# A two-role hybrid layer on eight cores: the split of the sequence moved from row 2176 to 2240, tiles of 64 rows at the ends of the roles, recurrent weights issued ahead of the branch, the last rows finished by halves

## The chip, the cores and the metric

One Trainium2 chip, one program on all eight cores, on two dies (cores 0 to 3 and 4 to 7). The time of a run is the device time of the slowest core, in microseconds (us). Some executions fall into a slower state, whatever the kernel: the cores of a die then show a lower granted TensorE clock. Such runs are marked slow and left out; all comparisons are between fast runs. In the traces PE is the matrix engine (TensorE), DVE the VectorE, ACT the ScalarE, POOL GpSimd and SP SyncE.

## The reference, cut to what matters

Four sequences of 4096 rows, 1024 channels, one layer:

```python
def reference(x, ...):                                   # x (4, 4096, 1024) float32
    h = rmsnorm(x, norm_mix)
    proj = h @ w_in                                      # u_pool | u_rnn | u_gate | g_merge (2 x 1024)
    y_pool = pool_mixer(u_pool, ...) @ w_pool_out
    v  = causal_depthwise_conv(u_rnn, conv_w, conv_b)    # 4 taps
    hr = rg_lru(v, ...)                                  # gates r, i from 128x128 blocks, then the scan below
    y_rnn = (hr * gelu(u_gate)) @ w_rnn_out
    x = x + (g_merge[0] * y_pool + g_merge[1] * y_rnn) @ w_o
    gu = rmsnorm(x, norm_ffn) @ w_ffn_in                 # 1024 -> 2 x 2816
    x = x + (silu(gate) * up) @ w_ffn_out
    return rmsnorm(x, norm_final)

# rg_lru: a_t = sigmoid(lam)^(8 r_t);  h_t = a_t h_{t-1} + sqrt(1 - a_t^2) (i_t v_t)
```

The scan over rows is what ties the two halves of a sequence together.

## The kernel before

Each sequence has two cores. The even core (first role) does rows 0 to T1 in two passes. The odd core (second role) cannot have the first role's recurrent state in time, so it computes it again: for rows 0 to T1 it redoes the norm, the recurrent projection, the convolution, the gates and the scan (the stage called "pre"), and then does all the work for rows T1 to 4096 in two passes. (cuts are marked `# ...`)

```python
T1 = 2176

CFG0 = {'role': 'a', 'P': 0, 'T': 2176,
        'passes': [{'T': 1152, 'rnn': [...], 'ffn': [384, 384, 384], 'groups': [11, 11], ...},
                   {'T': 1024, 'norm': [342, 342, 340], 'rnn': [342, 342, 340], 'mm': [512, 512],
                    'ffn': [512, 512], 'gch': [[0, 512], [512, 1024]], 'groups': [11, 11], ...}], ...}
CFG1 = {'role': 'b', 'P': 2176, 'T': 1920, 'pre': [256, 384, 768, 768],
        'passes': [{'T': 896, ...}, {'T': 1024, 'norm': [512, 512], 'rnn': [512, 512], 'ffn': [512, 512], ...}], ...}
```

The order of all instructions on all engines is not written by hand. Every operation is put down once with the buffers that it reads and writes; a scheduler in the program then simulates the engines and, where several operations could start, takes the one with the lowest rank. The ranks of some thousand operations of each role were found by a search with that simulation as the objective, and stand in the file as two packed tables:

```python
            tab = np.frombuffer(zlib.decompress(base64.b85decode(cfg["table"])), np.int32).reshape(2, -1)
            for o, r, q in zip(g.ops, *np.cumsum(tab, axis=1, dtype=np.int32)):
                o.rank = int(r) / 100.0
                o.gate = None if o.gate is None else int(q) / 100.0
        self.sched = Schedule(g, cfg["opts"])
```

One unit of the recurrence (one block of 128 channels by n rows; the names in the traces are those of the tiles here):

```python
        def rnn_unit(grp, j, wu, h, c0, n, rank, own, ...):
            # PE:   bu  = projection of h (n + 4 columns) by wu
            # ACT:  v   = first tap of the convolution
            # DVE:  v  += three more taps                     (L887 before, L928 after)
            # POOL: vb  = bf16 copy of v
            # PE:   ba, bx = two gates of vb                  (ps<-vb,rg)
            # ACT:  w = tanh(bx); a = tanh(ba); a = exp(a)    (L900, L903, L906; after: L941, L944, L947)
            # DVE:  w = (w + 1) * v
            # ACT:  v = a * a; v = sqrt(1 - v)                (tables: tanh, exp, sqrt)
            # DVE:  v = v * w; w = scan(a, v)                 (the scan of 768 columns takes 1.81 us, a product 0.96)
            # POOL: hst = last column of w
            # own rows only, DVE or POOL: gate the result into rt
```

The head of the program, the same for both roles, then the branch. The first body (near) is the second role's, the taken branch (far) goes to the first role's:

```python
        first_weights(range(2), -98)
        # ...
        norm_chunk(first, 16, 0, 256, -90, True, (1, 3, 5))
        g.pro = False                              # from here on: behind the branch
        g.grp = ("start",)
        first_weights(range(2, 8), -80)            # the other six recurrent weights
        load(cbr, dr["cbr"], 4096, -10)            # read by nobody in this configuration
        # ...
                e.br_eq(r, 0, far, near)
```

The end of the last pass, for each tile of 128 rows:

```python
                    for c in range(2):
                        bk = psum()
                        # PE:  11 matmuls, stationary Act[:, off:off+128], moving w2[:, c*512:(c+1)*512]
                        # DVE: X[t][:, c*512:(c+1)*512] += bk
                    if last:
                        rs = inv_root(X[t], ...)   # ACT square with sum over 1024 columns, two POOL steps
                        # DVE: X[t] = X[t] * rs * gF (1024 columns);  SP: store of X[t]
```

## Time and profile before

| | before |
|---|---|
| median of 3 runs | 1051.06 us (1047.61 to 1191.61; the last is a slow run) |
| spans of the even cores (first role) | 989.5 to 996.2 us, clock .985 to .989 |
| spans of the odd cores (second role) | 1041.9 to 1044.9 us, clock .966 to .968 |
| PE work of core 5, from the shapes (each matmul N / 2.4 GHz + 2.5 ns, a float32 one twice the N; warm-up matmuls left out) | 921.1 us |
| PE time lost on odd cores after the first matmul, mean | 96.9 us: 83.0 before 200 us, 13.9 after |
| the same on even cores, missing records added | 38.6 us |
| from the last matmul to the end, odd / even | 15.5 / 9.7 us |

"PE time lost" is the sum over all matmuls of (start of the next minus start of this, minus the work of this one): waits and slow clock together. (The float32 ones of 128 columns start 112 ns apart in the trace. The warm-up matmuls, which keep PE busy where it would stand, count as work here: 6.9 us on odd cores, 11.2 on even ones. Where a trace lacks records of matmuls, their work would count as lost; on two of the four even cores 67 are missing, 14.5 us by their shapes, and this is taken off.)

### The profile page before, as it was taken

What the parts mean: (1) busy time and instruction counts of PE and PEld (TensorE: products, weight loads), DVE (VectorE), ACT (ScalarE), POOL (GpSimd) and SP (SyncE); (2) the same over time, 40 slices, a digit from 0 to 9 for tenths busy, and PEclk for the clock granted to TensorE, in tenths of its full rate; (3) what the DMA queues carried; (4) which work ended last, traced back from release to release, by engine and by line L of the source; (5) the groups of instructions that cost most, each with busy time, mean ns of one, the idle gap of its engine ahead of it and who ended that gap; (6) DMA issues with size and microseconds to landing.
All of it is one profiled execution on the core that took longest, in us unless ns stands there. A gap on an engine that the chain in (4) does not pass through costs nothing.

```text
span 1044.9 us, 13923 instructions; the slowest of 8 cores (989.5 to 1044.9 us)
## 1 busy us (share of the span) xinstructions
PE 966.0 (92%) x5012; PEld 486.0 (47%) x5012; DVE 644.7 (62%) x935; ACT 522.8 (50%) x808; POOL 282.8 (27%) x528
## 2 busy tenths in 40 slices
PE   6766887699999999999999999999999999999994
PEld 4544543244454555544444554444444444444441
DVE  1778898869888863545967776444464333533343
ACT  4999978999956543348645453231224311200012
POOL 5253422426314334300133222112423221000001
PEclk9979898899999999999999999999999999999997
DMA  9944000726827599920078455438993494000013
GB/s 223 278 130 122 1 1 0 131 31 109 118 67 126 102 242 303 216 41 11 1 121 141 61 86 126 73 70 201 191 163 70 63 190 80 1 11 1 1 41 124
DMA packets 48927, 106.26 MB, mean 102 GB/s; under 512 B 5203, under 2 KB 7635, under 8 KB 48852
## 3 DMA queue, kind: packets, MB, share of 16 engines
q0 software_dynamic: 34848, 63.45, 37.0%
q1 hardware_dynamic: 14004, 41.83, 11.9%
q8 instruction: 44, 0.72, 0.3%
q14 instruction: 31, 0.25, 0.1%
HBM read 160.84 MB, written 7.86 MB: 161 GB/s over the span
## 4 chain that ended last, share of the span: by engine, by line
PE 75%; ACT 14%; DMA 5%; issue 2%; POOL 1%; DVE 1%; SPq 0%; POOLq 0%; ACTq 0%
PE ps L834 47%; PE ps L1227 13%; PE ps L1154 5%; PE ps L1116 5%; PE ps L1110 2%; ACT v L883 2%; ACT v L919 2%; ACT a L906 2%; ACT w L900 2%; ACT a L903 2%; DMA wu<-win 1%; ACT v L917 1%; DMA wo<-wo 1%; ACT L919 1%; DMA gr<-win 1%
## 5 line engine op out<-in xcount | busy, mean ns | idle before, releaser
L887 DVE SCALAR_TENSOR_TENSOR v<-ps,con,v 128x768 f32<-128x768 f32 (+4 forms) x192 | 136.7, 744 | 35.7 <-ACT v L883 34.3
L834 PE MATMUL ps<-h,fu 128*128 128x512 bf16 (+1 forms) x704 | 151.4, 366 | 0.0
L834 PE MATMUL ps<-h,fg 128*128 128x512 bf16 (+1 forms) x704 | 150.5, 366 | 0.4 <-DMA fg<-fi 0.3
L1227 PE MATMUL ps<-w,act 128*128 128x512 bf16 x660 | 145.9, 379 | 0.0
L1207 ACT ACTIVATE th<-ps 128x512 f32<-128x512 f32 (+1 forms) x88 | 50.1, 571 | 151.2 <-PE ps L834 148.9
L1210 DVE SCALAR_TENSOR_TENSOR th<-th,ps 128x512 f32<-128x512 f32 (+1 forms) x88 | 57.0, 652 | 84.5 <-ACT th L1207 84.2
L834 PEld LDWEIGHTS ps<-h,fu 128*128 128x128 bf16 x704 | 68.7, 98 | 72.8 <-issue 1.2
L834 PEld LDWEIGHTS ps<-h,fg 128*128 128x128 bf16 x704 | 68.4, 98 | 73.1 <-issue 2.0
L1227 PEld LDWEIGHTS ps<-w,act 128*128 128x128 bf16 x660 | 64.3, 98 | 77.0 <-issue 0.2
L692 ACT ACTIVATE junk<-X 128x1024 bf16<-128x1024 f32 x30 | 31.7, 1057 | 133.7 <-DVE X L1231 88.0
L891 POOL CAST vb<-v 128x768 bf16<-128x768 f32 (+4 forms) x64 | 47.1, 737 | 176.6 <-DVE v L887 175.9
L1231 DVE SCALAR_TENSOR_TENSOR X<-ps,X 128x512 f32<-128x512 f32 x60 | 41.4, 690 | 83.5 <-PE ps L1227 83.5
L923 DVE TENSOR_TENSOR_SCAN w<-a,hst,v 128x768 f32<-128x768 f32 (+4 forms) x64 | 80.1, 1276 | 0.4 <-POOL hst L926 0.3
L1213 DVE TENSOR_TENSOR act<-th,ps 128x512 bf16<-128x512 f32 (+1 forms) x88 | 56.5, 652 | 38.0 <-PE ps L834 36.9
L926 POOL COPY hst<-w 128x1 f32<-128x1 f32 x64 | 34.7, 543 | 146.1 <-DVE w L923 144.9
L834 PE MATMUL ps<-h,wu 128*128 128x452 bf16 (+3 forms) x448 | 70.1, 303 | 4.4 <-DMA wu<-win 3.0
L834 PE MATMUL ps<-hp,wu 128*128 128x260 bf16 (+2 forms) x320 | 64.6, 363 | 6.0 <-ACT a L903 2.1
L883 ACT ACTIVATE v<-ps,con 128x768 f32<-128x768 f32 (+4 forms) x64 | 49.4, 785 | 40.5 <-PE ps L834 29.0
L695 POOL TENSOR_SCALAR rs<-rs 128x1 f32<-128x1 f32 x62 | 16.6, 267 | 169.0 <-ACT junk L692 166.2
L834 PE MATMUL ps<-h,gp 128*128 128x448 bf16 (+1 forms) x256 | 56.4, 368 | 3.1 <-ACT tp L1106 1.7
L910 DVE SCALAR_TENSOR_TENSOR w<-w,v 128x768 f32<-128x768 f32 (+4 forms) x64 | 44.4, 696 | 22.6 <-ACT w L900 21.8
L1116 PE MATMUL ps<-R,ro 128*128 128x448 bf16 (+1 forms) x256 | 55.4, 366 | 1.8 <-DMA ro<-ro 1.8
(102 smaller groups left out, 1512.7 us busy)
## 6 DMA issues: line engine op xcount, KB each, us to landing
nat<-x SPq DMA_DIRECT2D x32, 512.0 KB, 9.8
fg<-fi POOLq DMA_DIRECT2D x44, 256.0 KB, 6.5
w<-fo POOLq DMA_DIRECT2D x44, 256.0 KB, 7.8
fu<-fi POOLq DMA_DIRECT2D x44, 256.0 KB, 8.4
X<-x SPq DMA_DIRECT2D x15, 512.0 KB, 6.1
out<-X SPq DMA_DIRECT2D x15, 512.0 KB, 4.2
wu<-win POOLq DMA_DIRECT2D x16, 256.0 KB, 9.8
ro<-ro POOLq DMA_DIRECT2D x16, 256.0 KB, 6.6
```

The source lines that it names most:

```text
L834: ins.append(e.matmul(ap(bk)[:, q:m], lhsT=ap(wt)[:, kc * 128:(kc + 1) * 128], rhs=ap(h)[:, kc, c0 + q:c0 + m], start=(kc == 0), stop=(kc ...
L883: g.op("act", lambda e: [e.activation(out=ap(v)[:], in_=ap(bu)[:, 1:1 + n], func=AF.Identity, scale=cwk(0), bias=ap(con)[:, C_CB + j:C_CB ...
L887: g.op("dve", lambda e, k=k: [e.scalar_tensor_tensor(out=ap(v)[:], in0=ap(bu)[:, 1 + k:1 + k + n], scalar=cwk(k), in1=ap(v)[:], op0=ALU.mu ...
L891: g.op("pool", lambda e: [e.tensor_copy(out=ap(vb)[:], in_=ap(v)[:])], r=[v], w=[vb], dur=d_pool(n), rank=rank + 0.4, tag="vb", two=True)
L910: g.op("dve", lambda e: [e.scalar_tensor_tensor(out=ap(w)[:], in0=ap(w)[:], scalar=1.0, in1=ap(vp)[:, 0:n], op0=ALU.add, op1=ALU.mult)], r ...
L923: g.op("dve", lambda e: [e.tensor_tensor_scan(out=ap(w)[:], data0=ap(a)[:], data1=ap(v)[:], initial=ap(hst)[:, j:j + 1], op0=ALU.mult, op1 ...
L1116: g.op("pe", lambda e: [e.matmul(ap(byr)[:, 0:n], lhsT=ap(wro)[:, j * 128:(j + 1) * 128], rhs=ap(Rt[j])[:, a:b], start=(j == 0), stop=(j = ...
L1154: g.op("pe", lambda e, bk=bk, t=t, c=c: [e.matmul(ap(bk)[:], lhsT=ap(Mx[m])[:, t * 128:(t + 1) * 128], rhs=ap(wo[m])[:, c * 512:(c + 1) * ...
L1207: g.op("act", lambda e, bg=bg, n=n, th=th: [e.activation(out=ap(th)[:], in_=ap(bg)[:, 0:n], func=AF.Tanh, scale=0.5)], r=[bg], w=[th], dur ...
L1210: g.op("dve", lambda e, bg=bg, n=n, th=th: [e.scalar_tensor_tensor(out=ap(th)[:], in0=ap(th)[:], scalar=1.0, in1=ap(bg)[:, 0:n], op0=ALU.a ...
L1213: g.op("dve", lambda e, bu=bu, n=n, th=th, at=at: [e.tensor_tensor(out=ap(at)[:], in0=ap(th)[:], in1=ap(bu)[:, 0:n], op=ALU.mult)], r=[th, ...
L1227: g.op("pe", lambda e, bk=bk, t=t, c=c, ci=ci, off=off, f0=f0, nf=nf, Act=Act, w2=w2: [e.matmul(ap(bk)[:], lhsT=ap(Act[f, ci])[:, off:off ...
```

## The change

The intent: the second role is the longer one by some 50 us, so 64 rows go from it to the first role. Since 2240 is no multiple of 128, the last tile of rows of each role has 64 rows. The start of the first role is helped by issuing the six later recurrent weights ahead of the branch, and the end of both by finishing the last tile in two halves. The model inside the scheduler was refined (a clock gate for PE, the real cost of the branch for the first role, two DMA queues that share), and both tables of ranks were searched anew. The core of the diff (tables, model and the many `[0:m_]` slices cut):

```diff
-T1 = 2176
+T1 = 2240
...
         norm_chunk(first, 16, 0, 256, -90, True, (1, 3, 5))
+        g.grp = ("start",)
+        first_weights(range(2, 8), -89)
         g.pro = False
-        g.grp = ("start",)
-        first_weights(range(2, 8), -80)
-        load(cbr, dr["cbr"], 4096, -10)
...
+        load(cbr, dr["cbr"], 4096, -10)
...
-            nt = TA // 128
+            nt = (TA + 127) // 128
+            rows = [min(128, TA - 128 * t) for t in range(nt)]
...
-                            ap(bk)[:], lhsT=ap(Act[f, ci])[:, off:off + 128], rhs=ap(w2[f - f0])[:, c * 512:(c + 1) * 512],
+                            ap(bk)[0:m_], lhsT=ap(Act[f, ci])[:, off:off + m_], rhs=ap(w2[f - f0])[:, c * 512:(c + 1) * 512],
...
+                    if last and pi == len(cfg["passes"]) - 1 and t == nt - 1:
+                        for c in range(2):         # square of each half as soon as it is there
+                            ...
+                        for c in range(2):         # scale and store each half
+                            ...
+                    elif last:
...
 CFG0: 
- 'T': 2176,
+ 'T': 2240,
-             'groups': [11, 11],
+             'groups': [8, 7, 7],                              (both passes)
-            {'T': 1024, 'norm': [342, 342, 340], 'rnn': [342, 342, 340], 'mm': [512, 512], 'ffn': [512, 512],
+            {'T': 1088, 'norm': [384, 384, 320], 'rnn': [364, 364, 360], 'mm': [384, 384, 320], 'ffn': [384, 384, 320],
 CFG1: 
- 'P': 2176, 'T': 1920, 'pre': [256, 384, 768, 768],
+ 'P': 2240, 'T': 1856, 'pre': [256, 384, 768, 832],
-            {'T': 1024, 'norm': [512, 512], 'rnn': [512, 512], ...
+            {'T': 960, 'norm': [512, 448], 'rnn': [480, 480], ...
 (new "opts" and new rank tables for both roles)
```

## The prediction

> **What bounds the kernel now.** I read the spans of the cores first, because the time is that of the slowest of eight.
>
> ```profile
> core 0: 989.5 us, clock 0.989
> core 1: 1041.9 us, clock 0.968
> core 2: 993.3 us, clock 0.987
> core 3: 1042.8 us, clock 0.968
> core 4: 991.1 us, clock 0.989
> core 5: 1044.9 us, clock 0.967
> core 6: 996.2 us, clock 0.985
> core 7: 1044.1 us, clock 0.966
> ```
>
> Even cores (first role, rows 0 to T1) end some 50 us before odd cores (second role: it redoes norm, recurrent projection, gates and scan for rows 0 to T1, the "pre" stage, then all work for the rest). The two dies are alike, so this is imbalance and not the slow state. Only a shorter second role shortens the kernel, and the first role can take about half of the 50 us before it is the bound.
>
> Second, the 40 slices of core 5 (26 us each):
>
> ```profile
> PE   6766887699999999999999999999999999999994
> DVE  1778898869888863545967776444464333533343
> ACT  4999978999956543348645453231224311200012
> PEclk9979898899999999999999999999999999999997
> ```
>
> The first eight slices have holes in PE while DVE and ACT stand at 8 to 9: there the pre stage is bound by these two. After that PE is full. Core 0 has such holes in its first two or three slices only.
>
> Third, what a matmul costs. Ends of matmuls are modelled, so I take starts. In the timeline of core 0:
>
> ```profile
> 434.30 9.66 PE L1227 MATMUL ps<-w,act 128*128 128x512 bf16 x44
> 443.79 0.31 PE L894 MATMUL ps<-vb,rg 128*128 128x342 bf16 x1
> ...
> 451.72 1.46 PE L834 MATMUL ps<-h,fu 128*128 128x384 bf16 x8
> 453.02 1.33 PE L834 MATMUL ps<-h,wu 128*128 128x344 bf16 x8
> ```
>
> (443.79-434.30)/44 = 215.7 ns for 512 columns; (453.02-451.72)/8 = 162.5 ns for 384. Both are N/2.4 GHz + 2.5 ns. With that, the list of shapes gives the PE work: 930 us on core 0, 921 us on core 5. Summing over the trace by which starts exceed this leaves, after the first matmul at 3.3 us, 36 us of lost PE time on core 0 (31 of it in the first 100 us) and 98 us on core 5: 84 in the first 200 us, 14 later.
>
> Fourth, starts, in the timelines: GpSimd of core 0, then of core 5.
>
> ```profile
> 8.02 0.54 POOL L625 DMA_DIRECT2D wu<-win  x1
> 18.25 1.70 POOL L625 DMA_DIRECT2D wu<-win  x3 [6.06 <-issue]
> ```
>
> ```profile
> 7.07 0.54 POOL L625 DMA_DIRECT2D wu<-win  x1
> 11.18 3.29 POOL L625 DMA_DIRECT2D wu<-win  x6
> ```
>
> The six later recurrent weights are issued behind the branch on the role. On core 0 GpSimd idles 6.06 us there and issues at 18.25; core 5 goes on at once at 11.18. On core 0 PE then waits 6.3 us in all for wu.
>
> **What the Trainium skill says.** (1) "TensorE: Matmul & The Clock Gate", section "Wait — 56ns, not 53.3ns?": start to start a warm matmul takes N / 2.4 GHz plus about 2.5 ns, a cold one N / 1.2 GHz. The trace agrees: 215.7 and 162.5 ns. So a chunk of 384 instead of 512 columns costs only the 2.5 ns more often. (2) Same page, section "LDWEIGHTS (loading the stationary operand)": its time follows the columns of the weights. Together: where the tile of rows is the stationary operand (W_o and the FFN output, 512 columns moving), 64 rows take the matmul time of 128. No run so far has a 64-row tile. (3) "Runtime: NRT & Kernel Launch", section "Instruction fetch mechanics": a taken branch to a target outside the fetched pages makes the engine fetch before it goes on. The 6.06 us on core 0 fits; core 5 falls into the near body and shows none. (4) "DMA: Bandwidth & Descriptors", section "Issuing engines are not separate DMA queues": an earlier issue gains only if the shared engines have room. In the first 25 us their share is 0.82 on core 0 and 0.94 on core 5, so there is a little room on core 0.
>
> **The change part by part.** *First role, pass 2 from 1024 to 1088 rows* (chunks 512,512 to 384,384,320), PE time:
> - FFN in, 352 weight blocks: 2 x 215.8 = 431.7 ns per block becomes 162.5 + 162.5 + 135.8 = 460.8 ns. +29.2 x 352 = +10.3 us.
> - gate, both merge gates and recurrent out, 256 blocks: +29.2 x 256 = +7.5 us.
> - pooling projection and its output (32 + 32 blocks): +1.9. Recurrent projection (64 blocks) and gates (16): 64 columns more each, +1.7 and +0.4.
> - W_o: a ninth tile of rows at full price, 16 x 215.8 ns = +3.5 us. FFN out: 44 x 215.8 ns = +9.5 us. Transposes and norm +0.4.
>
> Sum +35.2 us, all on PE, which has no room after 100 us. If 64 rows cost half on the last two it would be 6.5 us less.
>
> *Second role, pass 2 from 1024 to 960 rows*: FFN in -352 x 26.7 ns = -9.4; the 256 blocks -6.8; pooling two -1.7; recurrent projection -2.0 (480+4 columns fit one matmul, 512+4 needed two); gates -0.4. W_o and FFN out: eight tiles before, seven and a half after, so still eight matmul sets, 0. Sum -20.3 us on PE-bound ground.
>
> *Second role, pre stage plus 64 rows* (its last chunk 768 to 832). PE adds 3 us, but PE has holes there. DVE decides: three taps, two products and a scan at two columns' time is 7 times 64/960 us for each of 8 channel blocks, 3.7 us, and 0.3 for normed columns. ACT: six passes x 8 x 64 x 0.83 ns = 2.6, and one more tile of squares (1.06 + 0.19) and 0.2: 4.0. These two are filled to about 90%, so the stage ends +4 us later. Net for the second role -16.3 us.
>
> *Weights ahead of the branch*: first role only, issue about 6 us earlier. The wait of 6.3 us shrinks and part of the cold stretch after it (granted clock 0.73 from 25 to 50 us) goes with it, but the DMA bytes and DVE and ACT limit what follows. I take -5 of the 31 us lost there. Second role 0: it had no gap.
>
> *Last rows by halves*: today after the last matmul come 0.69 (add), 1.25 (square), 0.22 and 0.57 (GpSimd), 1.28 (scale), then a store. The square of the first half moves under the last matmuls: 512 x 0.83 ns = 0.4 us less. Scale and store in halves may gain some tenths for the store, but on core 5 the scale ends at 1033.8, the queue sees the store at about 1035.7 and then waits another 7.8 us for the closing barrier, where GpSimd's drain, 8.9 us, is the late one. So -0.5 us at most.
>
> *Moved without PE cost*: groups of 8, 7, 7 instead of 11, 11 FFN blocks in the first role add one add per half tile and pass: 18 x 0.69 = 12 us of DVE per pass, where DVE stands at 3 to 8 tenths: hidden. They free buffers earlier. New ranks reorder both programs, searched with a model of the clock gate and of the slow branch. After 200 us the second role loses 14 us of PE time, mostly to late weights (fg, ro, gr, wo); I give the new order 3 of these.
>
> Sum, slowest core of each role: first 996.2 + 35.2 - 5 - 0.5 = 1026; second 1044.9 - 16.3 - 0.5 - 3 = 1025. The two meet. The time of a run lay 1.6 us over the longest span (1046.52 against 1044.9), which makes 1027; as the search may find somewhat more I say **1026 us**.
>
> **The rivals.** (a) The first role becomes the bound: if the early weights bring nothing (DMA busy anyway) and the extra DVE adds delay its recurrent stage of pass 2, it is 996 + 35 + 3 = 1034, so about 1035 us. For it: DVE is at 21 to 22 of 25 us on core 0 from 425 to 475 us, where pass 1's FFN and the second recurrence overlap. Against it: PE lost almost nothing there. (b) The pre stage is what the second role waits for, and a larger last chunk (832 columns, two PSUM banks, longer scans) costs more than its share, some 8 us: second role 1030, time 1031. For it: the 84 us lost. (c) The reordering does more than the rebalance: the schedule was searched before without the real cost of the branch and without the clock. If the pre stage and the start give up 10 us each, about 1016. Against: DVE and ACT are truly full there, and no operation is taken from them. (d) Only the imbalance matters and 64-row tiles were free: 1020.
>
> **Range and chances.** Rebalance alone gives 1028 to 1031, the small parts take 2 to 8 off. Eight times in ten the time lies between 1016 and 1036. Two per cent below the fast runs of before (1047.6 and 1051.1, mean 1049.3) is 1028.3, just above my figure: faster by over 2% 0.55, within 2% 0.43, slower by over 2% 0.02, as that needs a mishap in the order on a role that has 20 us in hand.
>
> **What would show it.** Spans of even and odd cores within about 10 us of each other, even 1018 to 1030, odd 1018 to 1030. W_o and FFN out matmuls 288 and 792 on even cores (272 and 748 now) with 512 columns, starts still 216 ns apart in the 64-row tile. On the odd cores unchanged, 240 and 660. GpSimd's wu loads on core 0 all issued before 16 us, the wait for wu under 3 us. On odd cores PE full from about 203 instead of 199 us. The closing wait of some 8 us still there. It would be wrong if 64-row tiles ran their matmuls faster, if even cores gained new PE holes in the middle, or if the holes of the first 200 us on odd cores shrank by more than 5 us.

## More of the kernel before

The prediction shows the spans, the slices of core 5 and the timelines of the starts. Three more views of before are needed for the comparison later. First the PE waits of core 5 from 200 to 300 us. Columns: who waited, for whom, total us, times, longest.

```profile
PE ps L834 <- ACT tp L1106: 1.7, 1, 1.7
PE ps L834 <- ACT a L903: 1.3, 1, 1.3
PE ps L834 <- ACT w L900: 0.6, 1, 0.6
```

Once the pre stage is over, next to nothing stops PE. Second, where it ends, in the PE timeline of core 5 (start, us, what, count; in brackets the idle time before and what ended it):

```profile
184.19 2.77 PE L834 MATMUL ps<-hp,wu 128*128 128x512 bf16 x16 [1.32 <-ACT a L903]
...
195.09 0.80 PE L897 MATMUL ps<-vb,rg 128*128 128x512 bf16 x2 [5.85 <-ACT w L900]
...
198.85 2.65 PE L834 MATMUL ps<-h,wu 128*128 128x452 bf16 x8 [0.44 <-ACT w L900]
```

`hp` are the redone rows, `h` the role's own. The last redone projection is at 184 us; the first one of own rows (452 columns) comes just before the last redone gates. So on PE the two kinds of work hardly mix: its last gates of a redone unit are at 202 us, and its own projections begin at 199. (DVE goes on with redone scans to 261 us.)

Third, the first stretches of core 5 by engine (columns: stretch, its length, then busy time and number of instructions of PE, weight loads, DVE, ACT, POOL, then clock, DMA share, GB/s):

```profile
0.00:50.00 50.00, 35.95 (x227) 24.50 (x228) 24.09 (x59) 34.77 (x69) 20.84 (x51) 0.94 0.97 247
50.00:100.00 50.00, 35.21 (x200) 23.57 (x198) 39.78 (x67) 49.85 (x88) 20.35 (x44) 0.86 0.49 145
200.00:250.00 50.00, 49.42 (x257) 24.82 (x256) 38.93 (x50) 48.40 (x72) 13.72 (x23) 0.99 0.37 62
```

ACT is busy all the time from 50 to 100 us; PE is nearly full from 200 us on.

## The result, and the profile after

| | before | after |
|---|---|---|
| fast runs | 1051.06, 1047.61, 1047.11 us | 1037.28, 1037.87, 1035.3 us |
| slow runs | 1191.61 us | 1156.55 us (clock .86 to .87 on die 0) |
| median of all four | 1049.34 us | 1037.57 us |

The ratio of the fast runs is 0.989 (95% interval 0.985 to 0.993): faster, but by 1.1%, less than two per cent. Ratios here are computed as the mean time of one kernel's fast runs over that of the other's of the same rounds, so they are not quite the ratio of the medians.

The spans of the cores after:

```profile
core 0: 1026.8 us, clock 0.987
core 1: 1035.6 us, clock 0.970
core 2: 1026.7 us, clock 0.988
core 3: 1031.4 us, clock 0.974
core 4: 1028.6 us, clock 0.985
core 5: 1031.6 us, clock 0.975
core 6: 1028.9 us, clock 0.983
core 7: 1031.9 us, clock 0.975
```

The two roles have met, as intended. Over the fast runs the even cores have a mean of 1028.6 us and the odd ones 1032.4. In a later session with both kernels in the same rounds (told below) the first role grew by 39.5 us and the second fell by 11.7; against the kernel before of the other sessions (even 990.3 to 991.8, odd 1044.0 to 1045.9, three chips) the first session's means give about +37.7 and -12. Predicted were +29.7 and -19.8. Single odd cores spread with a standard deviation of 2.1 us, and the slowest of four sets the time: in fast runs after, the slowest odd core has a mean of 1035.2 us, and the run lasts 1.65 us longer than that.

The forty slices of core 5 after (25.8 us each):

```profile
PE   6677867688999999999999999999999999999994
...
DVE  2577798978989877433676875484435534334353
ACT  3999869989986535334573753251214322001011
PEclk9989998899999999999999999999999999999998
```

The PE row has two more slices below nine tenths than before: the ninth and the tenth, 206 to 258 us. DVE falls back in the second slice (5 for 7). The waits of PE on core 5 from 200 to 300 us:

```profile
PE ps L875 <- DVE v L928: 2.5, 1, 2.5
PE ps L875 <- DMA wg<-win: 1.9, 1, 1.9
PE ps L935 <- ACT w L941: 1.7, 1, 1.7
PE ps L935 <- ACT R L1039: 1.4, 1, 1.4
PE ps L938 <- DVE v L928: 1.2, 1, 1.2
...
```

With two more lines of 1.0 and 0.2 these are 9.9 us, where before had 3.6. And the PE timeline of core 5:

```profile
137.87 1.69 PE L875 MATMUL ps<-h,wu 128*128 128x452 bf16 x8 [1.63 <-ACT w L941]
...
213.93 0.51 PE L938 MATMUL ps<-vb,rg 128*128 128x512 bf16 x2 [1.16 <-DVE v L928]
...
224.50 1.67 PE L875 MATMUL ps<-h,wg 128*128 128x448 bf16 x8 [1.89 <-DMA wg<-win]
...
229.85 2.99 PE L875 MATMUL ps<-hp,wu 128*128 128x512 bf16 x16
...
```

The new order mixes the two kinds of units. The first own projection is at 138 us instead of 199, the last redone one at 230 instead of 184, and PE's last gates of a redone unit at 263 instead of 202. So PE's part of the redone units, for which it waits on DVE and ACT, now stands among the projections of own rows, which before ran almost without a wait. The prediction let the redone stage end 4 us later ("so the stage ends +4 us later"); its last scan ends at 291 us on core 5, where it ended at 261. The first stretches by engine:

```profile
0.00:50.00 50.00, 34.19 (x215) 24.16 (x215) 19.46 (x49) 32.21 (x62) 20.48 (x50) 0.97 0.83 193
50.00:100.00 50.00, 36.17 (x193) 23.04 (x194) 36.73 (x59) 49.88 (x92) 27.86 (x60) 0.86 0.32 115
200.00:250.00 50.00, 45.54 (x227) 22.21 (x228) 42.30 (x44) 45.83 (x62) 27.40 (x34) 0.94 0.55 85
```

By 100 us DVE has done 56.2 us of work instead of 63.9, and from 200 to 250 us PE is busy for 45.5 us instead of 49.4. The mean lost PE time of the odd cores: 83.6 us before 200 us (83.0 before the change), 12.7 from 200 to 300 (5.0), 8.6 later (8.9); in all 104.9 instead of 96.9. Most of the growth lies from 200 to 250 us: 7.9 us against 1.4.

The even cores: 45.8 us lost instead of 38.6, with the missing records taken off as above (here 42 on two of the four, 9.1 us). The first 250 us got better, 28.7 instead of 34.8; after 250 us the loss went from 3.8 to 17.1. (Warm-up matmuls, which count as work, fell by 4.6 us besides.) The longest PE waits of core 0 after 250 us, where the kernel before had a single one of 1.2 us:

```profile
PE ps L875 <- DMA wu<-win: 2.5, 1, 2.5
PE ps L875 <- DVE th L1252: 2.5, 1, 2.5
PE ps L1270 <- ACT tp L1147: 2.1, 1, 2.1
...
```

The tile of 64 rows, in the groups by shape of core 0 (columns: count, busy us, mean ns of one, idle before):

```profile
L1270 PE MATMUL ps<-w,act 128*128 128x512 bf16 x718 | 163.6, 379 | 3.9 <-ACT tp L1147 2.1 <-DVE act L1255 0.2 <-issue 0.2
L1196 PE MATMUL ps<-wo,mx 128*128 128x512 bf16 x263 | 60.0, 379 | 0.5
...
L1270 PE MATMUL ps<-w,act 128*64 128x512 bf16 x44 | 10.2, 380 | 0.0
...
L1196 PE MATMUL ps<-wo,mx 128*64 128x512 bf16 x16 | 3.8, 382 | 0.0
```

With 64 stationary columns a matmul takes what it takes with 128; the starts in the tile of 64 rows lie 216 ns apart too. (Loads of 64 weight columns took 110 ns on core 5, those of 128 columns 98: that the load time follows the columns, as the prediction's second point has it, isn't seen here.) The end of core 5:

```profile
1016.86 0.63 ACT L1285 ACTIVATE junk<-X 64x512 bf16<-64x512 f32 x1 [1.33 <-DVE X L1274]
...
1019.24 0.63 ACT L1285 ACTIVATE junk<-X 64x512 bf16<-64x512 f32 x1 [1.65 <-DVE X L1274]
...
1021.16 1.41 DVE L1299 SCALAR_TENSOR_TENSOR X<-X,rs,gF 64x512 f32<-64x512 f32 x2 [1.96 <-POOL rs L1293]
1021.98 1.14 SPq L1303 DMA_DIRECT2D out<-X  x2
```

The first half's square lies under the last matmuls, and only 0.63 us of square is left behind them (1.06 before). From the last matmul to the end odd cores now take 13.4 us (15.5 before), even ones 7.5 (9.7).

### The profile page after: what moved, and what is told of

Read it like the earlier page. It is cut to its first block, busy times and chain, and to the rows that moved or that the text cites. A ratio compares the mean times of both kernels' runs of the same rounds, so it can differ in the third digit from the quotient of the medians.

```text
span 1035.6 us, 13703 instructions; the slowest of 8 cores (1026.7 to 1035.6 us)
## 1 busy us (share of the span) xinstructions
PE 952.9 (92%) x4906; PEld 487.1 (47%) x4906; DVE 640.6 (62%) x936; ACT 512.4 (49%) x806; POOL 286.7 (28%) x529
## 3 DMA queue, kind: packets, MB, share of 16 engines
q1 hardware_dynamic: 13956, 41.04, 11.6%
## 4 chain that ended last, share of the span: by engine, by line
PE 67%; ACT 15%; DVE 6%; DMA 5%; issue 3%; POOL 3%; SPq 0%; POOLq 0%; ACTq 0%
PE ps L875 44%; PE ps L1270 11%; PE ps L1157 5%; PE ps L1196 3%; PE ps L1151 2%; DVE v L928 2%; ACT v L960 2%; ACT a L944 2%; ACT a L947 2%; ACT v L924 2%; DMA nat<-x 2%; ACT junk L732 2%; ACT w L941 1%; ACT v L958 1%; PE ps L808 1%
## 5 line engine op out<-in xcount | busy, mean ns | idle before, releaser
L928 DVE SCALAR_TENSOR_TENSOR v<-ps,con,v 128x480 f32<-128x480 f32 (+5 forms) x192 | 137.9, 744 | 28.9 <-ACT v L924 27.5
L875 PE MATMUL ps<-h,fg 128*128 128x512 bf16 (+2 forms) x704 | 146.5, 359 | 1.8 <-DMA fg<-fi 1.8
L875 PE MATMUL ps<-h,fu 128*128 128x512 bf16 (+2 forms) x704 | 147.0, 359 | 0.2
L1270 PE MATMUL ps<-w,act 128*128 128x512 bf16 (+1 forms) x660 | 146.7, 379 | 0.0
L1252 DVE SCALAR_TENSOR_TENSOR th<-th,ps 128x512 f32<-128x512 f32 (+2 forms) x88 | 55.4, 635 | 90.9 <-ACT th L1249 90.6
L1270 PEld LDWEIGHTS ps<-w,act 128*128 128x128 bf16 (+1 forms) x660 | 64.8, 99 | 77.1 <-issue 1.7
L1255 DVE TENSOR_TENSOR act<-th,ps 128x512 bf16<-128x512 f32 (+2 forms) x88 | 55.3, 635 | 57.2 <-PE ps L875 56.2
L964 DVE TENSOR_TENSOR_SCAN w<-a,hst,v 128x448 f32<-128x448 f32 (+5 forms) x64 | 81.2, 1283 | 0.2
L875 PE MATMUL ps<-hp,wu 128*128 128x512 bf16 (+3 forms) x320 | 66.6, 367 | 7.7 <-DVE v L928 4.0
L875 PE MATMUL ps<-h,wu 128*128 128x484 bf16 (+2 forms) x320 | 64.6, 347 | 6.5 <-ACT w L941 3.2
L967 POOL COPY hst<-w 128x1 f32<-128x1 f32 x64 | 28.7, 449 | 127.3 <-DVE w L964 126.0
L875 PE MATMUL ps<-h,wg 128*128 128x448 bf16 (+1 forms) x256 | 56.3, 369 | 2.6 <-DMA wg<-win 2.5
L951 DVE SCALAR_TENSOR_TENSOR w<-w,v 128x480 f32<-128x480 f32 (+5 forms) x64 | 44.5, 697 | 20.5 <-ACT w L941 20.4
```

What stands on the lines that cost most here:

```text
L875: ins.append(e.matmul(ap(bk)[:, q:m], lhsT=ap(wt)[:, kc * 128:(kc + 1) * 128], rhs=ap(h)[:, kc, c0 + q:c0 + m], start=(kc == 0), stop=(kc ...
L928: g.op("dve", lambda e, k=k: [e.scalar_tensor_tensor(out=ap(v)[:], in0=ap(bu)[:, 1 + k:1 + k + n], scalar=cwk(k), in1=ap(v)[:], op0=ALU.mu ...
L951: g.op("dve", lambda e: [e.scalar_tensor_tensor(out=ap(w)[:], in0=ap(w)[:], scalar=1.0, in1=ap(vp)[:, 0:n], op0=ALU.add, op1=ALU.mult)], r ...
L964: g.op("dve", lambda e: [e.tensor_tensor_scan(out=ap(w)[:], data0=ap(a)[:], data1=ap(v)[:], initial=ap(hst)[:, j:j + 1], op0=ALU.mult, op1 ...
L1252: g.op("dve", lambda e, bg=bg, n=n, th=th: [e.scalar_tensor_tensor(out=ap(th)[:], in0=ap(th)[:], scalar=1.0, in1=ap(bg)[:, 0:n], op0=ALU.a ...
L1255: g.op("dve", lambda e, bu=bu, n=n, th=th, at=at: [e.tensor_tensor(out=ap(at)[:], in0=ap(th)[:], in1=ap(bu)[:, 0:n], op=ALU.mult)], r=[th, ...
```

## The experiments

Where the second role's missing eight us went had several candidates, and the runs were chosen between them.

- **The order** (the theory that stood at the end): the searched order mixes own units with redone ones and does more of ACT's other work early. The redone stage ends later, and its waits stop PE at 200 to 300 us, where PE would have been full.
- **The size**: the last redone chunk of 832 columns costs more than its share of 4 us.
- **The front**: the dead load `cbr` and early squares of the role's own rows hold up ACT and DVE in the first 100 us.
- **The weights**: gate weights are issued later (201 us against 183 on core 5), and PE waits for them.
- **The crowd**: the early recurrent weights compete with the second role's first rows for the DMA engines.

Each run is told as the mean span of even and odd cores over its fast runs, beside the kernel before of the same rounds (b) or the changed kernel's own first session (even 1028.6, odd 1032.4). The mean of the odd cores of one kernel has a standard error of 0.2 to 1.1 us, so differences under about 1 us decide nothing. Kernels that compute something wrong are marked; they must be read with more care: in one of them, told below, cores whose code is unedited ran at a clock of 0.983 instead of 0.986.

### Early weights put behind the branch again (correct, ratio 0.990)

```diff
+        for o in self.sched.order["pool"][9:16]:     # the six wu loads and the rest of rg
+            o.pro = False
```

> The changed kernel with six of the eight recurrent weight tiles and the second piece of the gate weights issued after the branch again, in the same order, as in the kernel before; nothing else is touched. My step said that their place ahead of the branch is worth 5 us to the first role and nothing to the second. Expected if that holds: even cores 5 us longer (mean of the profiled spans 1027.8 to about 1033), odd cores within 1 us of 1032.6. Rival C (the early weights crowd the second role's start and cause its lost time): odd cores 3 us or more shorter.

Measured: even 1032.0 (+3.4), odd 1032.7 (+0.3); b 990.3 and 1044.0. GpSimd of core 0 in the changed kernel, then in this one:

```profile
11.21 0.63 POOL L665 DMA_DIRECT2D wu<-win  x1
12.36 2.65 POOL L665 DMA_DIRECT2D wu<-win  x5
```

```profile
18.63 0.63 POOL L665 DMA_DIRECT2D wu<-win  x1 [5.71 <-issue]
19.79 2.65 POOL L665 DMA_DIRECT2D wu<-win  x5
```

The branch's 5.71 us stand in front of the loads again, and PE of core 0 then waits 9.4 us for wu in the first 60 us, against none in the changed kernel. The three runs told below on the same chip in the same rounds, which leave the first role as it is in the changed kernel, have even cores of 1028.2 to 1029.2, some 3.2 us less than here. So the early issue is worth some 3.4 us to the first role, and no effect on the second is seen: the crowd falls. Because the slowest core is an odd one, it is worth next to nothing to the time (ratio 0.990 against 0.989).

### The last tile finished whole (correct, ratio 0.990)

```diff
-                    if last and pi == len(cfg["passes"]) - 1 and t == nt - 1:
+                    if False:
```

> The changed kernel with its last row tile finished whole (one square over 1024 columns, one scale, one store), as in the kernel before; the rest untouched. My prediction had given the halves 0.5 us. In the traces the time from the last matmul to the end of the span fell by about 2 us on both roles (odd cores 15.5 to 13.4, even cores 9.7 to 7.5). If the halves made that: all cores 2 us longer (odd 1032.4 to about 1034.4, even 1028.6 to about 1030.6). If it came from the smaller last tile of 64 rows instead: 0.5 us or less.

Measured: even 1029.2 (+0.5), odd 1033.7 (+1.2); b 991.4 and 1045.2. In its trace the square behind the last matmuls is again one of 1.06 us on 64 rows, as half the rows don't make an ACT instruction shorter. The traces decide how much of the shorter end is due to the halves, since the spans are from two sessions and their differences near the error: from the last matmul's start to the end it is 13.9 us on odd cores and 8.0 on even ones, against 13.7 and 7.7 with halves. So the halves give 0.2 to 0.3 us of the some 2 us by which the end got shorter; the rest was not taken apart. (GpSimd's closing drain, told at the end, is as short here as in the changed kernel.)

### The dead load moved to 200 us (correct, ratio 0.990)

```diff
-        load(cbr, dr["cbr"], 4096, -10)
+        load(cbr, dr["cbr"], 4096, -10, gate=(200 if P else None))
```

In the second role's table only the rank and the gate of this load change. In the changed kernel its queue issues `cbr` and then stands for 3.6 us before the next rows are loaded.

> The changed kernel with one load moved: the convolution bias row, which no instruction of either role reads, is issued late by the second role instead of fourth, right ahead of the 384-row chunk's row loads; every other instruction keeps its place and its address, and the first role is untouched. In the changed kernel the first of those row loads waits 3.6 us for the dead load to land and the row loads leave at 8.3 to 9.0 us, against 4.0 in the kernel before; VectorE is then 3 to 4 us behind at 35 to 55 us. Theory A (the new order costs the second role its gain): the row loads leave at about 5 us, the odd cores get 2 to 4 us shorter (mean of the profiled spans 1032.6 to about 1029.5) and the even cores stay within 0.5 us of 1027.8. Rival B (64 more rows in the recurrence's last chunk cost about 8 us by themselves): no change on the odd cores. Rival C (the early weights crowd the start): the row loads leave earlier but land no sooner, so no change either.

Measured: even 1029.2, odd 1031.7 with a standard error of 1.0; b 990.3 and 1044.0. In the trace the first scans end 2 to 3 us earlier (the fourth at 52 us instead of 55, the thirteenth at 107 instead of 110), and so do most up to 300 us, and the lost PE time is 101.9 us instead of 104.9; the spans gained only 0.7 us, which isn't told from nothing.

### The last redone chunk worked on 64 columns less (ratio 0.988)

```diff
+            thin = [v, vb, a, w]
+            if grp[:2] == ("pre", 3):
+                n = n - 64                       # views of these four tiles, same order, same buffers
```

The state that the second role starts from then skips 64 rows, which is wrong by design; the decay of the recurrence keeps the outputs within tolerance.

> The changed kernel with the recurrent units of the second role's last redone chunk working on 768 of their 832 columns; all tiles, addresses and the order stay as they are. The result is wrong on purpose (64 rows are left out of the recurrence). From the rows of the trace one unit saves some 64 columns on each of 6 ScalarE and 7 VectorE instructions, so about 4 us of each engine over 8 units, and about 2 us of TensorE. Theory A (the order, not the size, costs the gain): the odd cores get at most 4 us shorter, the price that I had put on the size (1032.6 to about 1029). Rival B (the size itself costs about 8 us, through waits that it lengthens): the odd cores get about 8 us shorter, 1032.6 to about 1025. Even cores unchanged.

Measured: even 1028.2, odd 1030.5, that is 2.0 us less than the changed kernel, or 1.8 if each is taken against the kernel before of the same rounds (-13.5 here, -11.7 in the session told below). The prediction gives 64 columns in this stage 4 us. They are worth less than that, not more: PE's work fell by 2.1 us, and its lost time stayed (104.7 us). Nothing here speaks for a chunk that costs 8.

### Seven early squares of own rows cut to 16 columns (wrong, ratio 0.988)

```diff
-            rs = inv_root(nats[t], rank, "sq1")
+            rs = inv_root(nats[t], rank, "sq1", w=16 if P and P <= 128 * t < P + 896 else D)
```

ACT of core 5 does 23 squares of rows in the first 100 us, against 17 before the change.

> The changed kernel with the squares of the seven row tiles that belong to the second role's own first pass cut from 1024 columns to 16; the order stays. The result is wrong on purpose (those rows get a wrong norm). In the changed kernel ScalarE is busy without a break from 25 to 100 us and executes 23 squares in the first 100 us, where the kernel before had executed 17; each takes about 1.1 us. Theory A (these squares were pulled ahead of the recurrent units and starve VectorE, which falls from 3 us behind at 75 us to 7.7 behind at 100): VectorE catches up some 5 us by 100 us and the odd cores get 4 to 6 us shorter, 1032.6 to about 1028. Rival B (the size of the last chunk): no more than 1 us. Even cores unchanged.

Measured: even 1029.0, odd 1030.6 (1.9 less than the changed kernel); b 990.3 and 1044.0. ACT is freed of some 6 us (an estimate: seven squares of 1.06 us, less what is left of them), and a third of it comes out at the end, not the 4 to 6 us expected.

### The three together (wrong on purpose, ratio 0.981, by the record unclear)

The three edits above in one kernel.

> The first three edits together: the dead load issued late, the recurrent units of the last redone chunk on 768 of 832 columns, the seven early squares of the second role cut to 16 columns. The result is wrong on purpose. Alone they had moved the mean span of the odd cores, over all fast runs, from 1032.4 us to 1031.7, 1030.5 and 1030.6: by 0.7, 2.0 and 1.9. If the three are separate small costs, they add up: 4 to 5 us, to about 1028. If each one alone was masked by the other two (an engine that is freed waits for the next late one), the three together give 8 us or more, to 1024 or less, and the whole of what my prediction missed on the second role is explained. If less than 4 us, the lost time is elsewhere (in the order of the recurrent units and of the projections between 200 and 300 us). Even cores within 1 us of 1028.6.

Measured, with five rounds: even 1025.7, odd 1026.4; b 991.4 and 1045.2. Three of its six runs were slow; the other three agree within 3 us. The odd cores gain 6.0 us over the changed kernel, somewhat more than the three singles add up to (0.7 + 2.0 + 1.9 = 4.6), the even ones 3, which none of the edits explains: with the squares alone, which carry the same wrong scale, they were at 1029.0. So part of the 6.0 may not be the edits' either. With the second role relieved by that much it ends where it was predicted. But relief is not the cause: the squares and the dead load are work that the kernel before did as well, and the 64 columns are in the prediction's sum already.

### The kernel before with 4 us more in the last redone chunk (correct, ratio 1.005)

Where the new chunk of 832 columns does 4 us more on ACT and DVE, the kernel before is given as much by cutting instructions in pieces: the overhead of an instruction comes more often, the result stays the same.

```diff
-            g.op("act", lambda e: [e.activation(out=ap(w)[:], in_=ap(bx)[:, 0:n], func=AF.Tanh, ...)],
+            cut = lambda k: [(n * i // k, n * (i + 1) // k) for i in range(k)] if grp[:2] == ("pre", 3) else [(0, n)]
+            g.op("act", lambda e: [e.activation(out=ap(w)[:, p:q], in_=ap(bx)[:, p:q], func=AF.Tanh, ...) for p, q in cut(3)],
...      (the tanh of a in 2 pieces, the product on DVE in 7)
```

> The kernel before, with three instructions of each of the eight units of the second role's last redone chunk cut into pieces (two tanh into 3 and 2, one multiply into 7): the same arithmetic and order, but by the fixed cost of a piece (about 0.15 us on ScalarE, 0.085 on VectorE, from durations of the same instruction at 256 and 768 columns, less the overlap of neighbours) some 3.6 us more on ScalarE and 4.1 us more on VectorE, about what the 64 rows add there. Correct result. Theory A (work in this stage is passed on at most one for one): odd cores 2 to 4 us longer, 1044.0 to about 1047. Rival B (the stage multiplies added work, so that 4 us cost 8): about 1052. Even cores unchanged.

Measured: even 989.4, odd 1049.0; b 991.4 and 1045.2. In its trace the eight units take about 3.5 us more of ACT and 3.3 us more of DVE (eight times 1.37 us for seven pieces instead of 0.96 for one), and the odd cores are 3.8 us longer: one for one. In the trace it is lost late: 2.2 us more before 200 us and 3.3 more from 200 to 250 us (4.7 instead of 1.4). So a longer stage costs PE time in that stretch in the old order too. This is the cleanest test of the prediction's step "so the stage ends +4 us later", and of the size as the cause: there the step holds, and with the narrowed chunk in the new order the size falls. (Even cores, whose code is unedited, were 1.9 us shorter here; so differences of that size can come without a cause in the edit.)

### The kernel before with the squares cut (wrong, ratio 1.002)

The same edit as above, in the old order, as a control.

> The control for the cut squares: in the kernel before, the squares of the seven row tiles of the second role's own first pass are cut from 1024 columns to 16, order untouched. Wrong result on purpose. In the changed kernel the same cut made the odd cores 1.1 us shorter against the runs of the kernel before of the same rounds, and with the two other edits the sum was 6.5 us. Theory A (it is the new place of these squares, ahead of recurrent units, that costs): in the kernel before the cut gives less, at most 1 us. Rival B (any work taken off ScalarE in this stage is passed on one for one, wherever it stands): 7 squares of 1.06 us, so up to 7 us shorter in the kernel before as well.

Measured: even 994.8, odd 1048.2; b 991.8 and 1045.9. No gain. Both roles got 2 to 3 us longer, the even cores too, whose code is the same as before, at a clock of 0.983 instead of 0.986. So the wrong data alone may cost a little, and the run only shows that cutting squares brings nothing in the old order, which does six fewer of them in the first 100 us. It also warns that the two runs above with this edit may understate their gain.

### The gate weights not waited for (wrong, ratio 0.987)

Projections of the second role's own first pass (in the first role, of both passes up to its last recurrent unit) take `rg`, which is long there, as their weights, and drop the wait for the load; the loads and the order stay.

```diff
-                    ins.append(e.matmul(ap(bk)[:, q:m], lhsT=ap(wt)[:, kc * 128:(kc + 1) * 128],
+                    ins.append(e.matmul(ap(bk)[:, q:m], lhsT=(ap(rg)[:, kc, 0:128] if id(wt) in other
+                                                              else ap(wt)[:, kc * 128:(kc + 1) * 128]),
```

> The changed kernel, with its projections reading weights that have been on the chip for long (the gate weights) in place of their own: in the second role all projections of its first own pass (56 groups of matmuls, at about 200 to 350 us), in the first role those of both passes that precede its last recurrent unit (162 groups), its second recurrent input among them. All loads are still issued, nothing waits for them there. Wrong result on purpose; order, addresses and the number of matmuls stay. In the profile of the changed kernel the weights of the second role's first projections are issued at 200.8 to 223 us (before: 182 to 198 us), TensorE waits 1.9 to 2.5 us for one of them, and 7.7 us more than in the kernel before between 200 and 300 us; on the first role it waits some 4 us for weights at 250 to 350 us. Theory A1 (late weights are what the new order costs): odd cores 4 us or more shorter, even cores 4 us shorter. Theory A2 (TensorE waits in any case for the recurrent units that now stand between the projections): odd cores at most 2 us shorter.

Measured: even 1030.0, odd 1032.3; b 991.8 and 1045.9. The waits for `wg` are gone from the view of PE waits, and the lost PE time of the odd cores is 104.7 us instead of 104.9: from 200 to 300 us it is 11.3 instead of 12.7, before that 0.8 more. Against the kernel before of the same rounds the second role is 13.6 us shorter, 1.9 more than in the change itself (11.7), with an error of about 1. So late weights carry some 2 us of it or less, not the eight. On even cores too the loss between 250 and 350 us stayed (8.9 us in this run, 8.3 in the changed kernel).

### Another order of the same work (correct, ratio 0.987)

With the dead load late, the ranks of both roles were searched once more, with an objective closer to what the traces show. No operation is added, removed or resized; about 60% of the second role's instructions stand at another place in their engine's order.

> The changed kernel, same split, same tiles, same work, correct result; other ranks for both roles, found by a search from the changed kernel's own (about 60 percent of the second role's instructions stand at another place in their queues), and the dead load late. Theory A (the order carries the lost time): the same work in another order changes the odd cores by 3 us or more in either direction, and if the search has hit what matters they get shorter: 1032.4 to about 1027. Rival B (what counts is the amount of work, whichever order): odd cores within 1 us of the run with the dead load late, 1031.7. Even cores, 1028.6: 1 us shorter or the same.

Measured, with five rounds: median 1034.8 us, even 1029.2, odd 1029.8; b 991.4 and 1045.2. The odd cores are 2.6 us below the changed kernel's (3.7 if each is taken against the kernel before of the same rounds), 1.9 below the run with the late load alone, and the lost PE time is 101.3 us instead of 104.9. It still does 23 early squares and mixes the units in much the same way; the scans up to 300 us come earlier by 0.9 to 4.4 us in the mean of a core. So order alone seems to move the second role by some us at the same work. But the comparison is between sessions on two chips, so it was made once more:

### A further searched order, and the changed kernel itself, on one chip (both correct, ratios 0.985 and 0.990)

The gain of the order before was read across sessions and chips. So a further searched order of the second role (about a third of its instructions change places against the kernel before this one; first role as there, same work) ran in the same rounds as an unedited copy of the changed kernel. Against the kernel before this one there is no diff but the packed table and the last digits of one constant of the scheduler; against the changed kernel there is the late load too, worth 0.7 us above.

> The order of the earlier searched kernel (same work, dead load late), with the second role's ranks searched a little longer; about a third of its instructions change places once more, the first role is as there. If the order is what costs the second role its missing time, and not one lucky draw of it, the odd cores again lie 2 to 4 us below the changed kernel of this same call (mean span 1028 to 1030 against about 1032), with the even cores at 1029. If the earlier gain was a matter of that chip or of chance, the odd cores of the two kernels agree within 1 us. PE time lost on odd cores: 100 to 102 us against 105.

> The changed kernel itself, as a control on the same chip and in the same rounds. Even cores 1028 to 1030, odd cores 1031.5 to 1033.5, ratio to the kernel before 0.987 to 0.990. If chips alone explain what was read as the gain of another order, this control moves to 1030 on the odd cores too.

| same chip, five rounds | kernel before | the change | further order |
|---|---|---|---|
| median, us | 1050.64 | 1039.35 | 1034.32 |
| fast runs | 12 | 6 | 5 |
| even cores, mean span | 991.2 | 1030.7 | 1030.4 |
| odd cores, mean span | 1046.1 | 1034.4 | 1028.9 |
| PE time lost, odd cores: up to 200 us / later | | 83.8 / 22.0 | 82.9 / 17.8 |

The odd cores are 5.5 us shorter by order alone (the place of the dead load is part of it), with standard errors of 0.4 each; the control did not move down with them. That is more than the 2 to 4 expected, and the control is at 1034.4, not 1031.5 to 1033.5, so part of it is a slower chip than that of the first session; but the difference is between kernels of the same rounds. Most of the gain lies after 200 us, but little of it where the change had lost most: from 200 to 250 us PE loses 7.3 us, against 8.0 in the control and 1.4 in the kernel before. From 250 to 300 us it is 2.8 against 4.7, later 7.1 against 8.6. PE waits of core 5 from 200 to 300 us in the further order:

```profile
PE ps L875 <- DVE v L928: 2.5, 1, 2.5
PE ps L875 <- DMA wg<-win: 1.3, 1, 1.3
PE ps L875 <- ACT R L1039: 1.0, 1, 1.0
PE ps L938 <- DVE v L928: 0.6, 1, 0.6
PE ps L875 <- DMA gr<-win: 0.3, 1, 0.3
```

5.7 us, against 8.3 in the control's core 5 (means of the four odd cores 7.1 and 9.1). Against the kernel before the second role is now 17.2 us shorter, which is near the predicted 19.8. This kernel beats both: 1034.3 us is 1.5% below the kernel before and 0.5% below the change.

### What could not be tried

The plain test of the order would be the new split with the old order, or the old split with the new. By the author's account, neither could be built: carried over by position, the old order of the second role gets the scheduler stuck for lack of buffers or gives a program that waits far more than either. The groups of 11, 11 with 1088 rows get stuck in the same way, and early weights in the kernel before need both tables made anew, as the head of the program is shared. The cost of the order is therefore known from where the waits lie and from other orders of the same work, not from a swap with the old one.

## Why the prediction was right or wrong

The mechanism was right (the second role is the bound, the split evens the roles out, no tile of 64 rows is cheap), the direction was right, and the time came out 11.6 us above the predicted 1026, 1.6 us beyond the end of the range. Of these, 2.1 are the start (the profiled execution of the kernel before lasted 1046.5 us, its three fast ones 1048.6 in the mean) and 0.8 the median of four, which counts the slow run. The fast runs' mean fell by 11.8 us, where the prediction's figures had said 20.5. By its own steps, for the second role:

| term | predicted | measured |
|---|---|---|
| PE work (pass 2 -20.3, pre stage +3) | -17.3 | -17.8, from the shapes |
| pre stage waits, up to 200 us (the stage +4, of it 3 PE work) | +1 | +0.6 |
| "I give the new order 3 of these" (waits after 200 us) | -3 | **+7.4** (13.9 to 21.3) |
| the end | -0.5 | -2.1 |
| sum | -19.8 | -11.9 |

The spans of the profiled runs fell by 10.8 us; the terms leave out 0.9 us more of warm-up matmuls.

**The step that failed** is "After 200 us the second role loses 14 us of PE time, mostly to late weights (fg, ro, gr, wo); I give the new order 3 of these." The search was taken for something that can only win. But it was a new search for a new problem, with another model, and it landed in an order that moves redone units past 200 us. Those 14 us did not become 11 but 21, all of the growth between 200 and 300 us. The prediction's own view of before held a warning: DVE and ACT at 8 to 9 tenths in the pre stage have little room, so their order can decide when PE is set free (an argument; no run tests it by itself). And the sentence on what would be seen, "PE full from about 203 instead of 199 us", is refuted by the timeline: PE has holes until about 262 us.

What is shown of this failure: where the time is lost (the waits, the timeline), that it isn't the size of the chunk (the kernel before with more work, the narrowed chunk), for the larger part not the late weights, not the crowd on the DMA engines, and that order alone moves the second role by 5.5 us at the same work in the same rounds. What is only argued: that the larger part of the eight us is the order's, and that mixing the units is the feature that costs. For it speak the place of the waits and the fall of the others. But the better order mixes as much (PE's last redone gates at 259 us on core 5) and wins mostly elsewhere, so the 6.5 us that appeared from 200 to 250 us were not won back: every run with the new split loses 6.5 to 8.5 us there. A longer stage lost 3.3 us more there in the old order as well, without the mixing, and no order with the two kinds apart was measured for the new split. Whether any order would have given the 3 us of gain that were booked stays open too.

**The first role** was mis-sized by as much and in the same way, but it cost little, since in the mean it still ends before the second. PE work +35.2 predicted, +34.9 from the shapes: right, with the tile of 64 rows at full price as said (rival d falls). Early weights -5, measured -3.4 by undoing them: of the right kind, and a little small. (The first 250 us lost 6.1 us less. The cold stretch that was to shrink with the wait did not: the clock of the even cores from 25 to 50 us is 0.63 to 0.71, and was 0.70 to 0.85.) The end -0.5, measured -2.2; of it the halves are 0.3, so that term was right in itself. But "They free buffers earlier" and "hidden" for the groups and chunks left out what the new kernel adds after 250 us: 13.3 us of lost PE time, with the waits shown above on weights and on `th`, `tp`. No run separates order, groups and chunks there. The prediction's list of what would make it wrong names it: "if even cores gained new PE holes in the middle". They did.

**The rivals.** (a) said 1035 and came nearest in number, but not in cause: the first role is not the bound (1028.6 against 1032.4), and its early weights did bring 3.4 us. (b), a last chunk that costs 8 us, falls, as shown. (c), a better order, which takes 10 us each from the pre stage and the start, fell for this order: the pre stage of the second role lost 83.6 us against 83.0, the first 250 us of the first role 6.1 less. The further order shows that some of it was to be had. (d), cheap tiles of 64 rows, fell. A rival's figure that fits is no proof of its cause.

**The chances.** Faster by over 2% had 0.55, within 2% had 0.43. The range held the rebalance with everything else at its best guess, and no case in which a searched order loses. With the order's term at 0 plus or minus 8 the time would have been 1029 plus or minus 8, and the chance of over 2% below a half.

## What to carry to other kernels

Count the work that a change moves and trust the sum: the PE terms came out within half a us. Do not book a gain for a new instruction order, searched or not; book a spread on both sides (here order alone moved a role by 5.5 us). When a gain goes missing, compare where each engine's lost time lies in time before blaming the part of the change that looks largest; then test that part by adding it, alone, to the old kernel.

## What the Trainium skill lacked or had wrong

- "ScalarE: Activation LUTs", section "What ACT_TABLE_LOAD costs", gives about 1283 ns for the load plus about 1380 ns of drain, some 2.66 us for each switch. The load's 1.28 us agrees; the drain isn't seen, before the load or after it. At 49 of the 51 loads of core 5 after the change the next instruction starts 1.29 to 1.30 us after the load does (the other two are followed by a longer wait), and the whole gap between the instructions around them is at most 1.31 us:

```profile
193.55 1.28 ACT L960 ACT_TABLE_LOAD   x1
194.85 3.20 ACT L960 ACTIVATE v<-v,misc 128x768 f32<-128x768 f32 x4
198.05 1.28 ACT L941 ACT_TABLE_LOAD   x1
199.35 0.95 ACT L941 ACTIVATE w<-ps,par 128x832 f32<-128x832 f32 x1
```

- "Runtime: NRT & Kernel Launch", section "Instruction fetch mechanics", says that a taken branch costs a fetch, but not how long. GpSimd stood for 4.6 to 6.1 us on the four even cores of the kernel before (6.06 on core 0) and 5.71 us on core 0 of the run with the weights behind the branch; with the loads ahead of it the first role gained 3.4 us. That the stand is this fetch fits, and no run shows it.
- "TensorE: Matmul & The Clock Gate", section "Seeing it yourself", says that on the default power profile a die goes to 13/16 of its clock once three of its cores run dense matmuls, and stays there while the load lasts. (Which profile was set here isn't on record.) Here eight cores run dense matmuls for a millisecond, and in fast runs their mean granted clock was 0.96 to 0.99. Only in slow runs one die fell, to 0.80 to 0.81 in one (1215.3 us, of the three together), which is near 13/16, but also to 0.83 to 0.90 or 0.93 to 0.95 in others. So in these runs a lower clock of a die was a state of some executions, not the rule.
- No page has a duration for the drain of GpSimd with which these programs end (the DRAIN record of POOL in the trace): 8.92 us before and 8.18 after on core 5, 7.07 and 4.85 on core 0, which is over half of the time between the last matmul and the end.
